# A recurrence whose running minima are spread over the partitions once for all heads, and gates computed as narrow columns

## The chip, the cores and the metric

One core of a Trainium2 chip runs the whole program in one launch. The metric is the device time of that launch in microseconds (us). The engines named below are TensorE (PE, with its weight loads as PEld), VectorE (DVE), ScalarE (ACT), GpSimd (POOL) and SyncE (SP), which issues the weight DMAs.

## The reference, cut to what matters

The model is two layers of one kind (attention, pooling, MLP, on 256 tokens and 256 context tokens) and then two layers of another kind on the 256 tokens, width 1024. The change lies in the second kind alone. Such a layer projects the normalised input to 9232+1024 columns, runs a differential attention with 8 heads (A) and an mLSTM with 8 heads (B), gates both and adds them to the stream. For B the gates are 16 of the projected columns, and the reference is

```
b = cumsum(log_sigmoid(f_pre)); d_log = b[t] - b[s] + ig[s]  (s <= t)
m_t = max(m_prev + b, max_s d_log)
scores = (q @ k.T) * exp(d_log - m_t)
h = (scores @ v + ...) / max(|sum(scores) + ...|, exp(-m_t))
```

It is written by chunks there; the kernel computes the same thing over all 256 tokens at once. With c[s] = ig[s] - b[s], the exponent is c[s] minus the running maximum of c up to t, so that the kernel needs, per head, a column c (by s, on the partitions) and a row of running minima of -c (by t, along the free axis, the same on all partitions), plus a mask that forbids s > t.

## The kernel before, in words

All matrix products of the projections are made in three passes: each float32 matrix is split into a rounded float32r part h and a rest l, and `mm3` (lines 426 to 430) adds l*h, h*h and h*l in PSUM. Weights come as 512 KB pieces in an order that `_order()` writes out (lines 140 to 191); five raw buffers hold them (`RAW`), ScalarE rounds them to `wh` (line 345), VectorE makes the rest `wl` (line 346), and four pieces may stand ready (`RING`). A piece of kind "raw" is taken unsplit and keeps its raw buffer until `W.finish`. The order of the instructions on each engine is made when the program is built, by the framework's scheduler with a simulated timeline and the order of the program text as priority.

The main stream of a layer is `in2(g, ...)`: twenty groups of 512 columns, each with two accumulators of 128 tokens, 8 steps of 2 x 3 matmuls of 512 columns (`group`, lines 479 to 494). After each step `tick()` lets the side generators (class `Sides`) put in a piece of their own work: the attention (lines 1539 to 1602), the gate chain (1477 to 1521), the convolutions (1624 to 1639), the recurrence (1689 to 1741), and `gate_T` (1747 to 1767), which normalises, gates and transposes an attention or recurrence result into the split operand (`oT`, `bT`) of the output products.

Gates (lines 1465 to 1475): the 16 gate columns are one weight piece of 8 steps of 16 columns, split into `wh` and `wl`; per step and token tile there are three matmuls with the activations as the 128x128 stationary operand and 16 columns moving, 48 in all. `chain_gates` turns them into `ccol` (c and exp of the running term, per token) and `nmm` (8 heads x 256 running minima, on 8 partitions).

Recurrence: `stage_s(h)` makes for one head the score products (lines 1698 and 1699, 64 rows of contraction, float32, 256 and 128 columns), and beside them, in a second PSUM bank, the exponent: a product of a one-hot column (`ident[0:8, h]` broadcast to 128) with `nmm` (line 1703, 8 rows, float32), which repeats that head's row on all partitions, and a product of the identity with the mask (line 1704) added to it. Two of each are needed, for the two blocks of s. `stage_e` takes the exponentials from PSUM with `ccol` as the bias (line 1711) and multiplies them with the scores (line 1713). `stage_v(h)`, two steps later, makes three matmuls with `vB` (line 1723), four small VectorE operations for the denominator (1727 to 1730) and two scaled copies into `hb` (1732). The recurrence runs beside `in2(14)`, `in2(12)`, `in2(15)` and `in2(13)`, and so does `gate_T` for the attention's result `oa`.

PSUM: `wk2()` is one buffer of two banks (tag `pr`), `wk_ps()` two buffers of one bank (tag `wk`), the accumulators take the remaining four banks. In SBUF the large tiles (`big`) share ten buffers; `gbuf` is one of them and is needed until the gate chain is done.

Of the kernel before, what the change touches and what calls it, by code (L numbers as in the profile page):

```python
# [26 lines left out]
def _units():  # L27
    u = []
    for i in range(2):
        for s in range(6):  # L30
            for e in range(8):
                u.append((("mod", i, s, e), 1024))
        for g, n in ((0, 416), (1, 448), (2, 448)):
            for h in range(2):
                u.append((("in", i, g, h), 4 * n))
        u.append((("uq", i), 1152))
        u.append((("ukv", i), 768))
        u.append((("pool", i), 128))
        for o in range(2):
            for h in range(2):  # L40
                u.append((("out", i, o, h), 2048))
        for f in range(16):
            u.append((("m1", i, f), 2048))
        for q in range(4):
            for o in range(2):
                for h in range(2):
                    u.append((("m2", i, q, o, h), 2048))
    for i in range(2):
        for g in range(20):
            for h in range(2):  # L50
                u.append((("in2", i, g, h), 2048))
        u.append((("gates", i), 128))
        for nm in ("oa", "ob", "oo"):
            for o in range(2):
                for h in range(2):
                    u.append(((nm, i, o, h), 2048))
    offs, at = {}, 0
    for key, n in u:
        offs[key] = (at, n)
        at += 128 * n  # L60
    return offs, at
# [26 lines left out]
_KC = [("ident", 128), ("mask", 128), ("maskT", 128), ("rope", 192), ("inv", 32), ("sel", 2), ("selg", 2)]  # L88
# [51 lines left out]
def _order():  # L140
# [41 lines left out]
    for i in range(2):  # L182
        def a2(*gs):
            return [("w", ("in2", i, g, h), 4) for g in gs for h in range(2)]
        o += a2(0) + [("w", ("gates", i), 8)] + a2(2, 4, 1, 3, 5)
# [9 lines left out]
def tile_kernel(ctx: ExitStack, tc: tile.TileContext, wp, xall, cols_d, rows_d, brow_d, con_d, band_d, pos_d, out):  # L195
# [91 lines left out]
    def cn(key, n):  # L287
        return con[:, _CON[key]:_CON[key] + n]
# [9 lines left out]
    maskr = const.tile([P, 4, P], F32R, name="maskr")  # L298
# [970 lines left out]
    S.copy(maskr[:, 0:4:2, :], cn("mask", 128).unsqueeze(1).to_broadcast([P, 2, P]))  # L1269
    S.copy(maskr[:, 3, :], cn("maskT", 128))  # L1270
# [104 lines left out]
    def second_layer(i, ent, nxt):  # L1375
# [87 lines left out]
        nmm = smp.tile([8, 256], F32, tag="nmm", name=nm("nmm"), bufs=1)  # L1463
        ccol = smp.tile([P, 2, 2, 8], F32, tag="ccol", name=nm("ccol"), bufs=1)
        pg = wk2()
        pgs = [pg[:, t, :] for t in range(2)]
        for k in range(8):
            w = W.kt(("gates", i))
            h, l = ent.view(k)
            for t in range(2):  # L1470
                mm3(pgs[t][:, 0:16], (h[:, t * P:(t + 1) * P], l[:, t * P:(t + 1) * P]), w, k == 0, k == 7)
            W.used()
        ug = gbuf[:, 0:32].rearrange("p (t g) -> p t g", t=2)
        for t in range(2):
            V.scalar_tensor_tensor(ug[:, t, :], pgs[t][:, 0:16], rs(t), rw("gb", 16), ALU.mult, ALU.add)

        def chain_gates():
# [6 lines left out]

            fT = ug[:, :, 8:16]
# [132 lines left out]


# [69 lines left out]
        def recurrence():  # L1689
            yield from until(h_gates, h_att1, *convs)  # L1690
            d = {}

            def stage_s(h):
                r0 = 64 * (h % 2)
                ft = h // 2
                pr = wk2()
                ps, pm = pr[:, 0, :], pr[:, 1, :]
                T.matmul(ps[:, 0:256], mqk[r0:r0 + 64, 4 + ft, 0:P], mqk[r0:r0 + 64, ft, 0:256], start=True, stop=True)
                T.matmul(ps[:, 256:384], mqk[r0:r0 + 64, 4 + ft, P:256], mqk[r0:r0 + 64, ft, P:256], start=True, stop=True)
                one = ident[0:8, h:h + 1].to_broadcast([8, P])  # L1700
                for s_ in range(2):
                    c0 = 256 * s_
                    T.matmul(pm[:, c0:c0 + 256 - P * s_], one, nmm[:, s_ * P:256], start=True, stop=False)  # L1703
                    T.matmul(pm[:, c0:c0 + P], identr, maskr[:, 3, :], start=False, stop=True)
                stage_e(h, ps, pm)

            def stage_e(h, ps, pm):
                wt = e4("wt")
                for s_ in range(2):
                    c0 = 256 * s_  # L1710
                    S.activation(wt[:, c0:c0 + 256 - P * s_], pm[:, c0:c0 + 256 - P * s_], AF.Exp, bias=ccol[:, s_, 0, h:h + 1])
                aT = wt[:, 512:1024]
                V.scalar_tensor_tensor(aT[:, 0:384], ps[:, 0:384], 0.125 * 0.25, wt[:, 0:384], ALU.mult, ALU.mult)
                d[h] = aT

            def stage_v(h):
                aT = d[h]
# [15 lines left out]
                del d[h]  # L1733

            for step in range(8 + 2):
                if 0 <= step - 2 < 8:
                    stage_v(step - 2)
                yield 1
                if step < 8:
                    stage_s(step)  # L1740
                yield 1
# [105 lines left out]
def _pack(a):  # L1847
# [46 lines left out]
    for i in range(2):  # L1894
# [9 lines left out]
        put(("gates", i), kt(w[:, 6144:6160]))  # L1904
# [50 lines left out]
    for j in range(4):  # L1955
        for s in range(2):
            con[32 * j + s, _CON["sel"] + s] = 1.0
            con[32 * j + s, _CON["selg"] + s] = 1.0
    con[2, _CON["selg"]:_CON["selg"] + 2] = 1.0
# [30 lines left out]
```

## Time and profile before

| | us |
|---|---|
| median of three runs | 1769.97 |
| lowest and highest run | 1767.61, 1774.82 |
| the profiled execution, its own time | 1766.66 |
| its span, first to last instruction | 1764.7 |
| mean granted TensorE clock, share of full | 0.984 |
| PE busy | 1694.5 (96%) |
| DVE busy | 1025.4 (58%) |
| ACT busy | 855.8 (48%) |
| POOL busy | 331.6 (19%) |

Busy time is the share of the span in which an engine had at least one instruction running. A matmul in the list lasts from its start to its modelled end, so neighbours overlap; the pace of a stream is read from the distances of the starts. A float32 matmul appears as two instructions, a float32r one as one.

### The profile page before, as it was taken

To read this page: it belongs to the slowest core of one execution; us is meant where nothing else is said; L and a number is where in the kernel's file an instruction comes from. 1 tells how busy PE (TensorE), PEld (TensorE's weight loads), DVE (VectorE), ACT (ScalarE), POOL (GpSimd) and SP (SyncE) were. 2 spreads that over 40 slices of the span, in tenths; PEclk is the share of its full clock that TensorE was granted. 3 is DMA by queue.
4 is the path that set the end of the run, shared out by engine and by line. 5 is a ranking of instruction groups with operands and counts; after the bars stand their busy time and mean duration, and the time that the engine had idled before them with its cause. 6 is when DMAs were issued, how large, how long until landed. Compare 5 with 4: busy or idle time off the path is not lost.

```text
span 1764.7 us, 26533 instructions
## 1 busy us (share of the span) xinstructions
PE 1694.5 (96%) x10062; PEld 1362.7 (77%) x10062; DVE 1025.4 (58%) x1882; ACT 855.8 (48%) x1658; POOL 331.6 (19%) x414
## 2 busy tenths in 40 slices
PE   6989999999999999889999999999999999999998
PEld 5776578777778888656899978877778788787787
DVE  3476634333333436774566778776575577866755
ACT  4556534413222234564544465665554446655542
POOL 1134110211112121331122224520000034300000
PEclk9999999999999999999999999999999999999999
DMA  7611254555443322602665545444355444343453
GB/s 285 211 61 54 74 190 125 179 163 166 149 151 118 96 78 77 219 30 81 218 189 184 188 146 167 138 132 156 119 170 188 145 155 154 129 160 119 155 183 104
DMA packets 71999, 256.23 MB, mean 145 GB/s; under 512 B 8120, under 2 KB 9272, under 8 KB 71616
## 3 DMA queue, kind: packets, MB, share of 16 engines
q1 hardware_dynamic: 71856, 254.53, 44.2%
q8 instruction: 79, 1.29, 0.3%
q14 instruction: 48, 0.39, 0.1%
q10 hardware_dynamic: 16, 0.02, 0.0%
HBM read 253.47 MB, written 1.05 MB: 144 GB/s over the span
## 4 chain that ended last, share of the span: by engine, by line
PE 86%; DVE 6%; ACT 3%; DMA 2%; POOL 2%; issue 1%; SPq 0%; DVEq 0%; ACTq 0%; POOLq 0%
PE acc L428 24%; PE acc L430 23%; PE acc L429 23%; PE acc L998 2%; DVE wl L346 2%; PE pr L549 2%; PE wk L1037 1%; DMA raw<-in_dram 1%; PE pr L1024 1%; ACT e L1011 1%; PE pr L1703 1%; PE wk L549 1%; ACT wh L345 1%; PE pr L1553 1%; DVE nmx L1008 1%
## 5 line engine op out<-in xcount | busy, mean ns | idle before, releaser
L346 DVE TENSOR_TENSOR wl<-raw,wh 128x1024 fp32r<-128x1024 f32 (+3 forms) x384 | 478.7, 1249 | 415.5 <-ACT wh L345 414.9
L345 ACT CAST wh<-raw 128x1024 fp32r<-128x1024 f32 (+3 forms) x384 | 396.7, 1034 | 505.2 <-PE acc L430 338.6
L428 PE MATMUL acc<-wl,hh 128*128 128x512 f32 x576 | 231.1, 401 | 4.6 <-ACT tga L1683 2.3
L429 PE MATMUL acc<-wh,hh 128*128 128x512 f32 x576 | 230.5, 400 | 0.0
L430 PE MATMUL acc<-wh,hl 128*128 128x512 f32 x576 | 229.6, 399 | 0.0
L428 PE MATMUL acc<-wl,hidh 128*128 128x512 f32 x384 | 152.5, 398 | 0.0
L429 PE MATMUL acc<-wh,hidh 128*128 128x512 f32 x384 | 151.2, 394 | 0.0
L430 PE MATMUL acc<-wh,hidl 128*128 128x512 f32 x384 | 151.0, 395 | 0.0
L1197 POOL TENSOR_TENSOR sqr<-relu 128x512 f32<-128x512 f32 (+1 forms) x64 | 72.6, 1135 | 346.5 <-ACT relu L1195 233.1
L428 PEld LDWEIGHTS acc<-wl,hh 128*128 128x128 f32 x576 | 109.5, 190 | 28.2 <-ACT tga L1683 3.2
L430 PEld LDWEIGHTS acc<-wh,hl 128*128 128x128 f32 x576 | 109.5, 190 | 22.8 <-issue 1.3
L429 PEld LDWEIGHTS acc<-wh,hh 128*128 128x128 f32 x576 | 109.5, 190 | 22.2 <-issue 1.3
L428 PE MATMUL acc<-hl,wh 128*128 128x258 f32 (+1 forms) x384 | 113.1, 295 | 3.5 <-DVE xc L1627 3.5
L429 PE MATMUL acc<-hh,wh 128*128 128x258 f32 (+1 forms) x384 | 111.6, 291 | 0.0
L430 PE MATMUL acc<-hh,wl 128*128 128x258 f32 (+1 forms) x384 | 111.0, 290 | 0.0
L428 PE MATMUL acc<-h2l,wh 128*128 128x512 f32 (+1 forms) x288 | 108.4, 376 | 2.7 <-DVE dx L1128 2.7
L429 PE MATMUL acc<-h2h,wh 128*128 128x512 f32 (+1 forms) x288 | 108.5, 377 | 0.0
L430 PE MATMUL acc<-h2h,wl 128*128 128x512 f32 (+1 forms) x288 | 107.5, 373 | 0.0
L428 PEld LDWEIGHTS acc<-wl,hidh 128*128 128x128 f32 x384 | 72.2, 188 | 17.8 <-issue 1.8
L430 PEld LDWEIGHTS acc<-wh,hidl 128*128 128x128 f32 x384 | 72.1, 188 | 17.1 <-issue 1.0
L429 PEld LDWEIGHTS acc<-wh,hidh 128*128 128x128 f32 x384 | 72.2, 188 | 16.4 <-issue 0.8
L1130 POOL TENSOR_TENSOR x<-x,dx 128x512 f32<-128x512 f32 x30 | 45.8, 1553 | 198.1 <-DVE dx L1128 198.1
(425 smaller groups left out, 3343.1 us busy)
## 6 DMA issues: line engine op xcount, KB each, us to landing
raw<-in_dram SPq DMA_DIRECT2D x448, 512.0 KB, 3.6
raw<-in_dram SPq DMA_DIRECT2D x16, 448.0 KB, 4.2
raw<-in_dram SPq DMA_DIRECT2D x8, 416.0 KB, 6.0
x<-in_dram SPq DMA_DIRECT2D x2, 1024.0 KB
band<-in_dram SPq DMA_DIRECT2D x4, 512.0 KB
raw<-in_dram SPq DMA_DIRECT2D x4, 288.0 KB, 4.2
out_dram<-x SPq DMA_DIRECT2D x4, 256.0 KB, 2.0
rows<-in_dram SPq DMA_DIRECT2D x4, 232.0 KB, 2.5
```

What stands on the lines that cost most here:

```text
L345: S.copy(h, src)
L346: V.tensor_tensor(l, src, h.bitcast(F32), ALU.subtract)
L428: T.matmul(ps, a[0], b[1], start=start, stop=False)
L429: T.matmul(ps, a[0], b[0], start=False, stop=False)
L430: T.matmul(ps, a[1], b[0], start=False, stop=stop)
L549: T.matmul(ps[32 * j:32 * j + 32, 0:P], cpad[:, k, :], raw[:, k * P:(k + 1) * P], start=a == 0, stop=a == 1)
L998: T.matmul(ps[:, a, s_ * w:(s_ + 1) * w], pr["q"][a][s_], pr["k"][a], start=True, stop=True)
L1008: V.tensor_reduce(nmx, ps.rearrange("p a (q w) -> p (a q) w", q=nq), AX.X, ALU.max, negate=True)
L1011: S.activation(e[:, c * w:(c + 1) * w], pf[:, c * w:(c + 1) * w], AF.Exp, bias=nmx[:, c:c + 1], accum_out=ssum[:, c:c + 1])
L1024: T.transpose(pt[:, a, (k * nq + s_) * P:(k * nq + s_ + 1) * P], d["e"][:, a * 512 + (s_ * nk + k) * P:a * 512 + (s_ * nk + k + 1) * P], i ...
L1130: (V if o else G).tensor_tensor(xs, xs, d, ALU.add)
L1197: G.tensor_tensor(s, t, t, ALU.mult)
```

## The change

The gate weights are padded from 16 to 32 columns and taken raw. They become the stationary operand: four steps of four matmuls with 32 columns of weights each, on the four column groups of the array, with 256 tokens moving (once the h part, once the l part of the activations). The four groups' partial sums lie on 4 x 32 partitions; they are copied out and added and transposed by two products with a small constant `self` (four stacked 16x16 identities), from which the old formula goes on.

A new generator `spread()` runs after the gate chain and the second half of the attention: it splits `nmm` into float32r parts and, for four heads at a time, makes the one-hot products (16 matmuls of 256 columns in all); VectorE adds the mask to the first 128 columns and ScalarE copies the others, into `gB`, a view of `gbuf`, which so stays in use until the last exponentials.

The recurrence works on pairs of heads: `stage_s(ft)` makes the score products of both heads, alternating between partitions 0 to 63 and 64 to 127 and between the two banks; VectorE adds the mask for the second block; ScalarE takes the exponentials from SBUF; one VectorE operation multiplies both heads. The products with the identity and the mask are gone, and the loop has five steps instead of ten.

```diff
-        o += a2(0) + [("w", ("gates", i), 8)] + a2(2, 4, 1, 3, 5)
+        o += a2(0) + [("raw", ("gates", i), 1)] + a2(2, 4, 1, 3, 5)

...
+        gB = gbuf.rearrange("p (h c) -> p h c", h=8)
-        pg = wk2()
-        pgs = [pg[:, t, :] for t in range(2)]
-        for k in range(8):
-            w = W.kt(("gates", i))
-            h, l = ent.view(k)
+
+        g_raw = []
+
+        def gate_weights():
+            g_raw.append((yield from W.take(("gates", i), 0)))
+
+        drain(spawn(gate_weights()))
+        g_w = g_raw[0].rearrange("p (k g) -> p k g", k=8)
+        pg = wk_ps()
+        for n in range(4):
+            for j in range(4):
+                k = 4 * (n // 2) + j
+                T.matmul(pg[32 * j:32 * j + 32, 0:256], g_w[:, k, :], ent.view(k)[n % 2][:, 0:256].bitcast(F32), start=n == 0, stop=n == 3)
+        W.finish(("gates", i), 0)
+        ug = gbuf[:, 0:32].rearrange("p (t g) -> p t g", t=2)
+
+        def gate_columns():
+            gs = gbuf[:, 768:1024]
+            S.copy(gs, pg[:, 0:256])
+            yield 1
+            pt = wk_ps()
-                mm3(pgs[t][:, 0:16], (h[:, t * P:(t + 1) * P], l[:, t * P:(t + 1) * P]), w, k == 0, k == 7)
-            W.used()
-        ug = gbuf[:, 0:32].rearrange("p (t g) -> p t g", t=2)
-        for t in range(2):
-            V.scalar_tensor_tensor(ug[:, t, :], pgs[t][:, 0:16], rs(t), rw("gb", 16), ALU.mult, ALU.add)
+                T.matmul(pt[:, 16 * t:16 * t + 16], gs[:, t * P:(t + 1) * P], cn("self", 16), start=True, stop=True)
+                V.scalar_tensor_tensor(ug[:, t, :], pt[:, 16 * t:16 * t + 16], rs(t), rw("gb", 16), ALU.mult, ALU.add)

...
+            yield from gate_columns()

...
+        def spread():
+
+            yield from until(h_gates, h_att1)
+            nmr = tmp(512, F32R, "nmr")[0:8, :].rearrange("p (b c) -> p b c", b=2)
+            split_into(nmr[:, 0, :], nmr[:, 1, :], nmm)
+            yield 1
+            for p4 in range(2):
+                pb = wk2()
+                for a in range(4):
+                    one = identr[0:8, 4 * p4 + a:4 * p4 + a + 1].to_broadcast([8, P])
+                    for b in range(2):
+                        T.matmul(pb[:, a // 2, 256 * (a % 2):256 * (a % 2) + 256], one, nmr[:, b, :], start=b == 0, stop=b == 1)
+                g4 = gB[:, 4 * p4:4 * p4 + 4, :]
+                b4 = pb.rearrange("p b (a c) -> p (b a) c", a=2)
+                V.tensor_tensor(g4[:, :, 0:P], b4[:, :, 0:P], cn("maskT", 128).unsqueeze(1).to_broadcast([P, 4, P]), ALU.add)
+                S.copy(g4[:, :, P:2 * P], b4[:, :, P:2 * P])
+                yield 2
+
+        h_spread = spawn(spread())
+

...
-            yield from until(h_gates, h_att1, *convs)
+            yield from until(h_spread, *convs)
-            def stage_s(h):
-                r0 = 64 * (h % 2)
-                ft = h // 2
-                pr = wk2()
-                ps, pm = pr[:, 0, :], pr[:, 1, :]
-                T.matmul(ps[:, 0:256], mqk[r0:r0 + 64, 4 + ft, 0:P], mqk[r0:r0 + 64, ft, 0:256], start=True, stop=True)
-                T.matmul(ps[:, 256:384], mqk[r0:r0 + 64, 4 + ft, P:256], mqk[r0:r0 + 64, ft, P:256], start=True, stop=True)
-                one = ident[0:8, h:h + 1].to_broadcast([8, P])
+            def stage_s(ft):
+
+                ps = wk2()
-                    c0 = 256 * s_
-                    T.matmul(pm[:, c0:c0 + 256 - P * s_], one, nmm[:, s_ * P:256], start=True, stop=False)
-                    T.matmul(pm[:, c0:c0 + P], identr, maskr[:, 3, :], start=False, stop=True)
-                stage_e(h, ps, pm)
-
-            def stage_e(h, ps, pm):
-                wt = e4("wt")
-                for s_ in range(2):
-                    c0 = 256 * s_
-                    S.activation(wt[:, c0:c0 + 256 - P * s_], pm[:, c0:c0 + 256 - P * s_], AF.Exp, bias=ccol[:, s_, 0, h:h + 1])
-                aT = wt[:, 512:1024]
-                V.scalar_tensor_tensor(aT[:, 0:384], ps[:, 0:384], 0.125 * 0.25, wt[:, 0:384], ALU.mult, ALU.mult)
-                d[h] = aT
+                    for a in range(2):
+                        r0 = 64 * a
+                        T.matmul(ps[:, a, 256 * s_:256 * s_ + 256 - P * s_], mqk[r0:r0 + 64, 4 + ft, P * s_:P * s_ + P],
+                                 mqk[r0:r0 + 64, ft, P * s_:256], start=True, stop=True)
+                wt = e4("wt").rearrange("p (a c) -> p a c", a=2)
+                V.tensor_tensor(wt[:, :, 256:384], gB[:, 2 * ft:2 * ft + 2, P:2 * P],
+                                cn("maskT", 128).unsqueeze(1).to_broadcast([P, 2, P]), ALU.add)
+                for a in range(2):
+                    h = 2 * ft + a
+                    S.activation(wt[:, a, 0:256], gB[:, h, :], AF.Exp, bias=ccol[:, 0, 0, h:h + 1])
+                    S.activation(wt[:, a, 256:384], wt[:, a, 256:384], AF.Exp, bias=ccol[:, 1, 0, h:h + 1])
+                V.scalar_tensor_tensor(wt[:, :, 0:384], ps[:, :, 0:384], 0.125 * 0.25, wt[:, :, 0:384], ALU.mult, ALU.mult)
+                d[ft] = wt
-                aT = d[h]
+                aT = d[h // 2][:, h % 2, :]

...
-                del d[h]
-
-            for step in range(8 + 2):
-                if 0 <= step - 2 < 8:
-                    stage_v(step - 2)
-                yield 1
-                if step < 8:
+
+            for step in range(4 + 1):
+                if step < 4:
-                yield 1
+                yield 2
+                if step > 0:
+                    for a in range(2):
+                        stage_v(2 * (step - 1) + a)
+                        yield 1

```

Left out above: the constant `self`, the padding of the weights from 16 to 32 columns (the piece grows from 64 to 128 KB) and the mask tile, which loses one of its four parts and the copy that filled it.

## Rows read from the trace of the kernel before

**Rows 1.** the page, parts 1, 4 and 6: engine, chain, weight DMA

```profile
PE 1694.5 (96%) x10062; PEld 1362.7 (77%) x10062; DVE 1025.4 (58%) x1882; ACT 855.8 (48%) x1658; POOL 331.6 (19%) x414
...
PE 86%; DVE 6%; ACT 3%; DMA 2%; POOL 2%; issue 1%; SPq 0%; DVEq 0%; ACTq 0%; POOLq 0%
...
raw<-in_dram SPq DMA_DIRECT2D x448, 512.0 KB, 3.6
```

**Rows 2.** timeline, PE, main stream; start us, us, engine, line, op, tiles

```profile
1204.94 0.39 PE L430 MATMUL acc<-wh,hl 128*128 128x512 f32 x1
...
1211.74 0.39 PE L430 MATMUL acc<-wh,hl 128*128 128x512 f32 x1
```

**Rows 3.** timeline, PE: first head of the recurrence

```profile
1213.10 0.39 PE L430 MATMUL acc<-wh,hl 128*128 128x512 f32 x1
1213.42 0.70 PE L1698 MATMUL pr<-mqk 64*128 64x256 f32 x2
...
1214.27 0.69 PE L1703 MATMUL pr<-nmm,con 8*128 8x256 f32 x2
1214.89 0.33 PE L1704 MATMUL pr<-maskr,identr 128*128 128x128 f32 x1
...
1215.72 0.45 PE L428 MATMUL acc<-wl,hh 128*128 128x512 f32 x1
...
1216.01 0.40 PE L429 MATMUL acc<-wh,hh 128*128 128x512 f32 x1
```

**Rows 4.** timeline, PE: gates, first and last of 48, and what follows

```profile
1054.78 0.17 PE L428 MATMUL pr<-wl,hh 128*128 128x16 f32 x1
...
1059.94 0.26 PE L430 MATMUL pr<-wh,hl 128*128 128x16 f32 x1
...
1060.05 0.61 PE L430 MATMUL acc<-wh,hl 128*128 128x512 f32 x1
```

**Rows 5.** behind the gates; us, PE, PEld, DVE, ACT, POOL busy, PEclk, DMA

```profile
1060.00:1064.00 4.00, 4.00 (x12) 3.18 (x12) 3.93 (x10) 3.49 (x4) 4.00 (x4) 0.57 0.51 165
1422.00:1426.00 4.00, 4.00 (x12) 3.22 (x12) 3.93 (x8) 2.22 (x3) 4.00 (x4) 0.57 0.17 46
```

**Rows 6.** timeline, PE: three products with vB amid the stream

```profile
1646.11 0.40 PE L428 MATMUL acc<-wl,hh 128*128 128x512 f32 x1
1646.35 0.83 PE L1723 MATMUL wk<-vB,wt 128*128 128x129 f32 x6
...
1647.25 0.39 PE L430 MATMUL acc<-wh,hl 128*128 128x512 f32 x1
```

**Rows 7.** timeline, PE: attention scores, two row groups amid the stream

```profile
1090.75 0.39 PE L429 MATMUL acc<-wh,hh 128*128 128x512 f32 x1
1091.07 0.70 PE L1553 MATMUL pr<-kT,qT 64*128 64x256 f32 x4
...
1092.03 0.39 PE L428 MATMUL acc<-wl,hh 128*128 128x512 f32 x1
```

**Rows 8.** timeline, PE: modulation products, four column groups amid the stream

```profile
314.02 0.40 PE L428 MATMUL acc<-h2l,wh 128*128 128x512 f32 x1
314.35 0.64 PE L549 MATMUL pr<-raw,cpad 128*32 128x128 f32 x16
...
315.26 0.39 PE L430 MATMUL acc<-h2h,wl 128*128 128x512 f32 x1
```

**Rows 9.** the same view: recurrence of layer 1, and a later stall of PE

```profile
1213.30:1276.10 62.80, 62.80 (x299) 48.43 (x299) 39.41 (x98) 34.28 (x64) 0.00 (x0) 1.00 0.37 123
...
1302.00:1308.00 6.00, 4.83 (x24) 3.68 (x23) 4.29 (x9) 4.26 (x8) 0.00 (x0) 1.00 0.55 174
```

**Rows 10.** groups by form, DVE, 1205 to 1330 us: the recurrence and gate_T

```profile
L1713 DVE SCALAR_TENSOR_TENSOR wt<-pr,wt 128x384 f32<-128x384 f32 x8 | 4.4, 556 | 11.6 <-ACT wt L1711 11.6
L1760 DVE SCALAR_TENSOR_TENSOR oa<-oa,rs,saz 128x128 f32<-128x128 f32 x16 | 4.4, 347 | 0.0
...
L424 DVE SCALAR_TENSOR_TENSOR oTl<-wk,gang,oTh 128x256 fp32r<-128x256 f32 x8 | 3.8, 475 | 0.0
```

More of the change, by code (lines that the diff above doesn't have):

```diff
@@ L51, in _units @@
                 u.append((("in2", i, g, h), 2048))
-        u.append((("gates", i), 128))
+        u.append((("gates", i), 256))
         for nm in ("oa", "ob", "oo"):
@@ L86 @@
     _NROW += _n
-_KC = [("ident", 128), ("mask", 128), ("maskT", 128), ("rope", 192), ("inv", 32), ("sel", 2), ("selg", 2)]
+_KC = [("ident", 128), ("mask", 128), ("maskT", 128), ("rope", 192), ("inv", 32), ("sel", 2), ("selg", 2), ("self", 16)]
 _CON, _NCON = {}, 0
@@ L297, in tile_kernel @@
     identr = const.tile([P, P], F32R, name="identr")
-    maskr = const.tile([P, 4, P], F32R, name="maskr")
+    maskr = const.tile([P, 3, P], F32R, name="maskr")
     ones = const.tile([P, P], F32, name="ones")
@@ L1268, in tile_kernel @@
     S.copy(identr, ident)
-    S.copy(maskr[:, 0:4:2, :], cn("mask", 128).unsqueeze(1).to_broadcast([P, 2, P]))
-    S.copy(maskr[:, 3, :], cn("maskT", 128))
+    S.copy(maskr[:, 0:3:2, :], cn("mask", 128).unsqueeze(1).to_broadcast([P, 2, P]))
     S.activation(maskr[:, 1, :], ident, AF.Copy, scale=0.0)
@@ L1903, in _pack @@
                     put(("in2", i, g, h), wk_[:, 4 * h:4 * h + 4])
-        put(("gates", i), kt(w[:, 6144:6160]))
+        put(("gates", i), kt(np.concatenate([w[:, 6144:6160], np.zeros((1024, 16), f32)], axis=1)))
         for nm_, key in (("oa", "w_out_a_2"), ("ob", "w_out_b_2"), ("oo", "w_o_2")):
@@ L1958, in _pack @@
             con[32 * j + s, _CON["selg"] + s] = 1.0
+        con[32 * j:32 * j + 16, _CON["self"]:_CON["self"] + 16] = np.eye(16, dtype=f32)
     con[2, _CON["selg"]:_CON["selg"] + 2] = 1.0
```

## Prediction, made before the changed kernel was run

> **What bounds the kernel now.** I read the page first: PE is busy 96% of the span and carries 86% of the chain that ended last [rows 1]. So a microsecond taken from PE's stream is worth about a microsecond, wherever PE doesn't wait, and the question is what the touched pieces cost that stream. The timeline answers it: the side work stands between the matmuls of the main stream, and the distance of the neighbours, less their own pace, is its price. The pace: 30 steps from 1204.94 to 1211.74 us, 0.2267 us for 512 columns in one pass, 0.443 ns a column [rows 2]. The second thing to see is the stretch table behind the gates, where the granted clock is 0.57 [rows 5]. The third is DVE in the recurrence, 39.4 of 62.8 us [rows 9], since DVE is what could take PE's place.
>
> **What a head costs now.** From the L430 at 1213.10 to the L429 at 1216.01 are 2.91 us [rows 3]; two steps of the stream lie in that (0.453), so the head's six products cost 2.46. Sixteen heads (8 in each of two layers): 39.3 us.
>
> **What the gates cost now.** 48 matmuls from 1054.78 to the next of the stream at 1060.05 [rows 4]: 5.27 us a layer, 0.110 us each though only 16 columns move. PE had no gap in it, and yet the clock behind is granted at 0.57 over 4 us in both layers [rows 5], that is partly at the 1.2 GHz level instead of 2.4: 4 x 0.43 = 1.72 us lost a layer.
>
> **Prices of the new products.** Float32, same shape of array as the stream: three products of 129 columns cost 1647.25 - 1646.11 - 0.453 = 0.69 us [rows 6], 1.77 ns a column, four times the stream's 0.443, and nothing on top. Row groups: two products of 256 columns on 64 rows each cost 1092.03 - 1090.75 - 0.453 = 0.83 [rows 7]; one alone would stream 256 x 1.77 = 0.45, so the two run together and 0.37 is paid for the visit. Column groups: eight products of 128 columns with 32 weight columns cost 315.26 - 314.02 - 0.453 = 0.79 [rows 8]; two rounds stream 0.45, so four run together, and the visit costs 0.33. That a visit with another shape costs about 0.35 and one with the same shape nothing fits a rule. The Trainium skill, "TensorEngine Tiling (Array Packing)", Tiling Modes, Key Properties, says that a change of the tiling mode drains TensorE; the trace agrees, with the 0.37 and 0.33 above. It speaks against this change, which makes 14 such visits of its own (8 for scores, 4 to spread, 2 for gates); without it the new work would come out some 5 us cheaper.
>
> **The change, part by part.**
> - Scores: eight pair visits instead of sixteen single ones, each (256 + 128) x 1.77 ns = 0.68, plus 0.37: 1.05, in all 8.4 us.
> - Spreading: 32 products of 256 columns in float32r, in four batches of eight: 8 x 256 x 0.443 ns = 0.91, plus 0.37 = 1.28; in all 5.1 us. A float32r product on 8 rows isn't in the trace. Below, it can't stream faster than the pace, and the batch could miss the 0.37 (3.6 in all); above, the float32 rate makes it 8 x 0.45 + 0.37 = 4.0 a batch, 16.0 in all. I take the low rate, since the operands have the type of the stream.
> - Masks by DVE: the sixteen mask visits are gone with the heads' 2.46.
> - So the recurrence gives 39.3 - 8.4 - 5.1 = 25.8 us. Products with vB and the transposes of gate_T stay, and as same-shape work cost nothing extra wherever they fall.
> - Gates: four rounds of 256 columns, 4 x 0.453 + 0.33 = 2.15 us; then two products of 16 columns, four instructions with 128 weight columns, by the narrow ones' 0.110 each 0.44 (if each made a visit of 0.37 of its own, 1.2). Per layer 5.27 - 2.15 - 0.44 = 2.7, and 1.72 for the clock if it doesn't fall: 4.4, two layers 8.8 us. Between nothing and 1.72 for the clock I take 1.72: the new gate products are of the kind of the modulation visits [rows 8], behind which the stream goes on at its pace (314.92 to 315.26 apart), than to the narrow ones.
> - Off the path: the split of the gate weights (ACT and DVE) goes, the piece grows to 128 KB. It now holds its raw buffer until PE has read it, and the loads behind it on SP's queue wait for that. Four split pieces stand ready, each 12 matmuls x 0.227 = 2.7 us of stream, 10.9 us, against 3.6 us to land [rows 1]. Without that cover: 3.6 us a layer.
> - New waits: the gate chain starts one copy later; its results aren't needed before the attention ends. The recurrence waits for the spreading, which has the last projection groups ahead of the recurrence to run beside; the second batch waits until DVE and ACT have emptied the first (under 1 us each by the 0.475 for 256 columns [rows 10]), with PE's stream going on. Both products with vB wait for one multiplication of both heads; four ticks lie between, some 5 us of stream, against about four exponentials and 1.1 us on DVE. If that is late, PE stands, with the whole stream behind it.
> - DVE in the recurrence: eight multiplications of 556 ns become four of at most twice that (no change), and four mask additions of about 475 ns come on top [rows 10]: 41.3 us. PE's stretch shrinks by 8 x 2.46 - 4 x 1.05 = 15.4 to 47.4 us, so DVE goes from 63% to 87%. In that state PE lost 6.0 - 4.83 = 1.17 us later [rows 9]; I book one more such stall a layer, 2.3 us.
>
> Sum: 25.8 + 8.8 - 2.3 = 32.3 us. The profiled execution took 1766.66 us, 3.3 less than the median of the runs shown. 1766.7 - 32.3 = 1734.4; against the median 1738.
>
> **The rivals.**
> - *DVE becomes the bound of the recurrence.* Over 47.4 us a layer, DVE's order fills up and gate_T's share, 16 x 0.347 + 8 x 0.475 = 9.4 us [rows 10], falls to PE as waits: 18.7 us instead of 2.3, 1754. For it: 87%, and splits for the stream in the same queue. Against it: four pieces stand ready, and gate_T isn't needed until the output product, four groups later. Chance 0.13.
> - *The groups don't run together* (the change doesn't do what it says): each pair 0.68 more, each gate stage 12 x 0.453 = 5.4 more: 5.4 + 10.9 = 16.3, 1754. Rows 7 and 8 show both together [rows 7, 8], so 0.04.
> - *The clock falls all the same*, behind the gates and behind the spreading too, in both layers: 4 x 1.72 = 6.9, 1745. Chance 0.08. The Trainium skill, "TensorE: Matmul & The Clock Gate", Part 1, puts a fall of the clock down to idleness; by that the gates, which left no gap, wouldn't be its cause, and 3.4 of these us would stay lost. The rows differ from it, as far as busy time shows.
> - *Slower: the buffers.* `gbuf` lives until the last exponentials. Beside it stand the two halves of the input, oa, mqk, vB, saz, hb and the gate tile: nine of ten; the first half of `oT` takes the tenth, so that the second finds no buffer until `gbuf` or `mqk` is free. If that comes later than `in2(19)`, both gate_T passes run alone in front of the output products: per head 2 x 0.347 + 2 x 0.475 = 1.64 one after the other, 13.2 a pass, 26.3 a layer, 52.6 in all: 34.6 - 52.6 = 18 slower, 1788. It decides only if the last pair slips past `in2(16)` to `in2(19)`, four groups of 48 x 0.227 = 10.9 us; with the recurrence some 47 us long it should be done before these begin. Chance 0.04.
>
> **How the numbers follow.** Forecast 0.71, the rivals 0.13, 0.04, 0.08 and 0.04. The forecast's own range is 1726 (no stall, float32r batches without the 0.37, hidden column products, run to run some us) to 1746 (a second stall, part of the spreading at the float32 rate). To leave out no more than 2 in 10 it reaches to 1753, most of the way to the DVE rival. Half a per cent, 8.8 us, is about what a measurement of this kernel can tell from no change. All cases but the last are over that; with mixtures of the DVE case: faster 0.92, within 0.04, slower 0.04.
>
> **What would show it.** Right: PE's busy time lower by about 30 us; a pair visit of about 1.05 us and a spreading batch of about 1.3 in the timeline; the gate stage near 2.6 us with the clock at 1.00 behind it; DVE above 80% in the recurrence, PE's waits up by a few us. Wrong: waits of PE for `wl` or `wt` of over 10 us; a pair visit near 1.7; or a first `oT` half that comes only after the recurrence, with PE standing at the output product.

## The result, and the profile after

The changed kernel took 1741.28 us in the median of four runs (1738.86 to 1744.13), the kernel before, beside it on the same chip, 1768.79 (1766.45 to 1774.82). The ratio on record is 0.9833, with a 95% interval from 0.9811 to 0.9856: faster by 1.4 to 1.9%, some 25 to 33 us (the two medians by themselves give 0.9844, 27.5 us). The forecast was 1738.0, the range 1726 to 1753.

The page of the profile of the changed kernel, parts 1 and 4, answers to [rows 1]:

```profile
span 1738.9 us, 26348 instructions
...
PE 1666.3 (96%) x9974; PEld 1341.6 (77%) x9974; DVE 1026.5 (59%) x1886; ACT 859.6 (49%) x1663; POOL 331.9 (19%) x414
...
PE 85%; DVE 6%; ACT 3%; DMA 2%; issue 2%; POOL 1%; SPq 0%; DVEq 0%; ACTq 0%; POOLq 0%
```

PE is busy 28.2 us less, and the bound is the same: 96% of the span, 85% of the chain. The timeline of PE in the changed kernel (start, length, engine, line, operation, tiles), first a spreading batch, then a pair of heads, answers to [rows 3]:

```profile
1208.46 0.39 PE L430 MATMUL acc<-wh,hl 128*128 128x512 f32 x1
1208.78 1.22 PE L1644 MATMUL pr<-nmr,identr 8*128 8x256 f32 x8
1209.93 0.50 PE L428 MATMUL acc<-wl,hh 128*128 128x512 f32 x1
1210.27 0.40 PE L429 MATMUL acc<-wh,hh 128*128 128x512 f32 x1
...
1216.87 0.39 PE L428 MATMUL acc<-wl,hh 128*128 128x512 f32 x1
1217.19 0.92 PE L1733 MATMUL pr<-mqk 64*128 64x256 f32 x8
1218.04 0.50 PE L429 MATMUL acc<-wh,hh 128*128 128x512 f32 x1
1218.38 0.40 PE L430 MATMUL acc<-wh,hl 128*128 128x512 f32 x1
```

Two steps of the stream (0.453) lie in each. The batch costs 1210.27 - 1208.46 - 0.453 = 1.36 us (forecast 1.28), the pair 1218.38 - 1216.87 - 0.453 = 1.06 (forecast 1.05); the other pairs and batches that stand by themselves cost the same within 0.01. The gates of layer 1, in the same view, answer to [rows 4]:

```profile
1054.74 0.39 PE L430 MATMUL acc<-wh,hl 128*128 128x512 f32 x1
1055.06 0.38 PE L1395 MATMUL wk<-lp,ones 64*128 64x2 f32 x2
1055.37 0.64 PE L1477 MATMUL wk<-hh,raw 128*32 128x256 f32 x8
...
1056.35 0.50 PE L428 MATMUL acc<-wl,hh 128*128 128x512 f32 x1
...
1057.02 0.42 PE L1477 MATMUL wk<-hl,raw 128*32 128x256 f32 x3
...
1058.71 0.42 PE L1477 MATMUL wk<-hh,raw 128*32 128x256 f32 x3
...
1060.04 0.39 PE L429 MATMUL acc<-wh,hh 128*128 128x512 f32 x1
```

The 16 products don't stand together: the scheduler put steps of the stream between them, so three visits pay the change of array shape. From 1054.74 to 1060.04 are 5.30 us; eight steps of the stream (1.81) and the older L1395 products (0.40, to 1055.37) lie in that. That leaves 3.1 us instead of 2.15; in layer 2 two visits cost 2.7. Behind them the clock is granted in full, where it was 0.57 [rows 5]; the stretch table of the changed kernel (us, busy PE, PEld, DVE, ACT, POOL, PEclk, DMA), the recurrence last, which answers to [rows 9]:

```profile
1060.00:1064.00 4.00, 4.00 (x19) 3.25 (x19) 1.94 (x6) 3.97 (x8) 2.20 (x5) 1.00 0.38 131
...
1408.00:1412.00 4.00, 4.00 (x20) 3.32 (x20) 4.00 (x6) 1.20 (x2) 4.00 (x4) 1.00 0.74 263
...
1213.30:1276.10 62.80, 62.80 (x321) 51.56 (x320) 47.96 (x116) 41.30 (x73) 0.00 (x0) 1.00 0.48 158
```

PE has no gap in the recurrence, though DVE rose from 39.4 to 48.0 us in a stretch of 62.8.

**A ledger without the start.** The medians hide where the difference lies, because the first layers, which the change hardly touches, take from 1035 to 1043 us from profile to profile. So each profile is cut where the third layer begins (the first L428 on `wl,hh`); behind that point, PE's idle time is summed over twenty equal stretches, and the clock loss as PE's busy time times (1 - PEclk). These sums are the measure of the experiments (us but for the ratio):

```
kernel                   median ratio  until cut  behind it  idle  clock loss
before                       -          1035.1     729.6     18.1    10.3
before again (e5)            -          1036.6     729.4     17.8    10.4
gates alone (e1)           0.9969       1039.8     723.4     19.2     6.2
recurrence alone (e2)      0.986        1040.3     702.6     15.8    10.6
after                      0.9833       1038.5     700.4     21.9     6.0
after again (e11)          0.9831       1037.5     700.7     19.2    10.3
softmax by ACT (e3)        0.9817       1038.4     700.0     18.1     8.1
head by head (e4)          0.9827       1040.3     702.8     21.0    10.4
mask by GpSimd (e6)        0.9823       1036.8     700.2     21.4     4.8
mask twice by DVE (e7)     0.982        1038.7     700.6     19.2    10.2
gates behind group 2 (e8)  0.9802       1041.6     697.8     18.9     9.3
e3 and e8 together (e9)    0.9763       1040.8     690.1     14.3     3.9
gates before group 5 (e10) 0.9765       1042.9     690.2     15.6     3.9
e3 and e10 together (e12)  0.9799       1041.8     693.6     18.3     2.5
```

The change is worth 29.2 us behind the cut, the forecast 32.3. Two profiles of the same program agree there within 0.3 us; idle time and clock loss trade against each other between them (21.9 and 6.0, 19.2 and 10.3), so only their sum is compared below. e4, whose products cost PE the same, stands 2.1 to 2.4 us above them, so a difference of that size between one profile each of two kernels shows nothing. What is called PE's waits in the attention and the convolutions below is its idle time from a layer's beginning to its first scores of the recurrence, without the waits for `hh` and `hl` at the beginning.

### The profile page after: what moved, and what is told of

It reads as the page before. It is cut to its first block, busy times and chain, and to the rows that moved or that the text cites. A ratio compares the mean times of both kernels' runs of the same rounds, so it can differ in the third digit from the quotient of the medians.

```text
span 1738.9 us, 26348 instructions
## 1 busy us (share of the span) xinstructions
PE 1666.3 (96%) x9974; PEld 1341.6 (77%) x9974; DVE 1026.5 (59%) x1886; ACT 859.6 (49%) x1663; POOL 331.9 (19%) x414
## 3 DMA queue, kind: packets, MB, share of 16 engines
HBM read 253.61 MB, written 1.05 MB: 146 GB/s over the span
## 4 chain that ended last, share of the span: by engine, by line
PE 85%; DVE 6%; ACT 3%; DMA 2%; issue 2%; POOL 1%; SPq 0%; DVEq 0%; ACTq 0%; POOLq 0%
PE acc L428 24%; PE acc L429 24%; PE acc L430 23%; PE acc L998 2%; PE pr L549 2%; DVE wl L346 1%; DMA raw<-in_dram 1%; PE wk L1037 1%; PE pr L1024 1%; ACT e L1011 1%; PE wk L549 1%; PE pr L1567 1%; ACT wh L345 1%; DVE nmx L1008 1%; PE wk L1752 1%
## 5 line engine op out<-in xcount | busy, mean ns | idle before, releaser
L346 DVE TENSOR_TENSOR wl<-raw,wh 128x1024 fp32r<-128x1024 f32 (+2 forms) x382 | 475.0, 1246 | 411.3 <-ACT wh L345 410.8
L345 ACT CAST wh<-raw 128x1024 fp32r<-128x1024 f32 (+2 forms) x382 | 395.8, 1037 | 491.4 <-PE acc L430 327.3
L428 PE MATMUL acc<-wl,hh 128*128 128x512 f32 x576 | 229.2, 398 | 3.6 <-ACT tga L1717 2.6
L428 PE MATMUL acc<-wl,hidh 128*128 128x512 f32 x384 | 152.7, 398 | 0.0
L428 PEld LDWEIGHTS acc<-wl,hh 128*128 128x128 f32 x576 | 108.3, 188 | 27.7 <-ACT tga L1717 3.1
L428 PE MATMUL acc<-hl,wh 128*128 128x258 f32 (+1 forms) x384 | 113.0, 294 | 1.2 <-DVE xc L1661 1.2
L428 PE MATMUL acc<-h2l,wh 128*128 128x512 f32 (+1 forms) x288 | 108.7, 377 | 2.7 <-DVE dx L1128 2.7
L428 PEld LDWEIGHTS acc<-wl,hidh 128*128 128x128 f32 x384 | 72.1, 188 | 17.7 <-issue 1.8
```

The source lines that it names most:

```text
L345: S.copy(h, src)
L346: V.tensor_tensor(l, src, h.bitcast(F32), ALU.subtract)
L428: T.matmul(ps, a[0], b[1], start=start, stop=False)
```

## The experiments

**e1, gates alone.** The kernel before with the gate part of the change.

```diff
-                mm3(pgs[t][:, 0:16], (h[:, t * P:(t + 1) * P], l[:, t * P:(t + 1) * P]), w, k == 0, k == 7)
...
+                T.matmul(pg[32 * j:32 * j + 32, 0:256], g_w[:, k, :], ent.view(k)[n % 2][:, 0:256].bitcast(F32), start=n == 0, stop=n == 3)
```

> The kernel before with the new gates alone (narrow columns, raw weights), the old recurrence. Theory A (the gates' gain is partly swallowed: PE reaches the convolutions earlier and waits there for a chain of GpSimd work that is as long as before): the clock is 1.00 behind the gates, but the time is only 2 to 5 us under the kernel before, PE standing 5 us or more a layer around the convolutions. Rival B (the gates earn all that was forecast, and the recurrence falls short because of VectorE): 8 to 9 us under the kernel before.

Measured: 1766.74 us against 1773.15, ratio 0.9969 (0.9952 to 0.9986), so 2 to 9 us; in the ledger 6.2. The interval spans both theories' numbers; the profile is clearer: clock loss 4.1 us lower, idle time 1.1 higher. PE's waits in the attention and the convolutions are 4.7 and 5.2 us in the two layers, 4.0 and 3.4 in the kernel before: theory A's picture, at about its size.

**e2, recurrence alone.** The kernel before with the spreading and the pairs.

```diff
-            yield from until(h_gates, h_att1, *convs)
+            yield from until(h_spread, *convs)
...
-                one = ident[0:8, h:h + 1].to_broadcast([8, P])
...
+                wt = e4("wt").rearrange("p (a c) -> p a c", a=2)
```

> The kernel before with the new recurrence and spreading alone, the old gates. Theory A: 24 to 26 us under the kernel before (ratio about 0.986), the clock behind the gates still near 0.57 for 4 us. Rival B: the recurrence is worth only some 19 us (0.989), with PE's waits in it up by 5 us or more.

Measured: 1747.71 us, ratio 0.986 (0.9832 to 0.9888), so 20 to 30 us; in the ledger 27.0. That is near theory A, and PE's idle time fell from 18.1 to 15.8 us, where the rival had it rise by 5. With the gates of 16 columns kept, the clock loss stays at 10.6. The stretches behind the gates in e2 show why:

```profile
1064.00:1068.00 4.00, 4.00 (x20) 3.47 (x20) 3.90 (x12) 2.52 (x3) 3.39 (x2) 0.69 0.36 135
1412.00:1416.00 4.00, 4.00 (x23) 3.61 (x24) 3.67 (x11) 1.84 (x3) 3.84 (x4) 0.71 0.40 131
```

and the same in e1:

```profile
1064.00:1068.00 4.00, 4.00 (x20) 3.34 (x20) 3.96 (x6) 3.42 (x6) 3.89 (x3) 1.00 0.38 120
1420.00:1424.00 4.00, 4.00 (x19) 3.33 (x18) 3.46 (x6) 2.77 (x4) 3.59 (x4) 1.00 0.81 251
```

The windows cut the lower stretch differently, so that the mean of 4 us is 0.57 in one kernel and 0.69 in the other. The level is the same: 0.50, that is 1.2 GHz, in e2 as between 1060.40 and 1063.60 us in the kernel before. Here is e2 up to the end of its gates and behind them:

```profile
1055.00:1065.60 10.60, 10.60 (x72) 9.46 (x71) 7.16 (x21) 7.23 (x11) 6.22 (x15) 1.00 0.38 129
1065.70:1068.90 3.20, 3.20 (x9) 2.55 (x8) 3.13 (x10) 3.17 (x4) 3.20 (x3) 0.50 0.31 95
```

So the lower clock goes with the old gate products of 16 columns, and goes away with them. A wait of 1.2 us for `hh` at the beginning of layer 1 went away with them too, but it isn't the cause: in layer 2 such waits (0.9 us for `hh`, 1.5 for `hl`) stand ahead of the gates in e1 as in e2. The Trainium skill, "TensorE: Matmul & The Clock Gate", Part 1, ties the clock to how busy TensorE has been recently. PE's busy time is 10.60 of the 10.60 us ahead of the lower stretch, so the rows differ from the rule as far as busy time shows.

**e4, another order of the score products.**

```diff
-                for s_ in range(2):
-                    for a in range(2):
+                for a in range(2):
+                    for s_ in range(2):
```

> The changed kernel with the score products of a pair issued head by head instead of alternating between the two row groups. If the row groups run together only when neighbours in the order lie on different groups: a pair visit grows from 1.06 to about 1.5 us (256 columns more of float32 stream), some 3.6 us in all over the changed kernel. Rival D (the groups run together whatever the order, or not at all): the visit stays at 1.06 and the time within 1.5 us.

Measured: 1743.79 us, ratio 0.9827 (0.9792 to 0.9861). The pair in e4's timeline:

```profile
1218.56 0.39 PE L428 MATMUL acc<-wl,hh 128*128 128x512 f32 x1
1218.88 0.93 PE L1733 MATMUL pr<-mqk 64*128 64x256 f32 x8
1219.74 0.50 PE L429 MATMUL acc<-wh,hh 128*128 128x512 f32 x1
1220.08 0.40 PE L430 MATMUL acc<-wh,hl 128*128 128x512 f32 x1
```

1220.08 - 1218.56 - 0.453 = 1.07 us, the same. The edit did reach PE: in the program as built the four products stand head by head. Yet between 1218.88 and 1219.41 us the view by form shows only products of 256 columns, which are the first ones of both heads (two instructions each):

```profile
L1733 PE MATMUL pr<-mqk 64*128 64x256 f32 x4 | 0.7, 428 | 0.0
```

So the second head's first product, third in order, runs beside the first head's, ahead of the first head's second one. The order of issue doesn't decide whether the two row groups run together, and they do: all eight instructions take 0.93 us, where 2 x (256 + 128) columns one after the other would stream 1.36. The ledger has e4 2.1 to 2.4 us above the changed kernel, all of it in idle time and clock loss (31.4 against 27.9 and 29.5); the medians show no difference.

**e5, the kernel before once more.**

> The kernel before, unchanged, profiled once more. Its first profile reached the second layers 3.4 to 5.2 us earlier than the profiles of the changed kernel and of its two halves, with a granted clock of 1.00 between 15 and 45 us where the others show 0.87 to 0.97. If that is scatter of the first stage from one execution to the next (theory A), this profile starts its first recurrent layer between 1036 and 1041 us, with a clock below 1.00 somewhere between 15 and 45 us. If the change itself disturbs the start (theory B), it is again at 1035 us with 1.00.

Measured: 1767.96 us; the third layer begins at 1036.6. The stretches of e5 at the start:

```profile
15.00:30.00 15.00, 12.48 (x94) 8.34 (x95) 11.25 (x38) 9.85 (x30) 5.26 (x16) 0.91 0.96 346
30.00:45.00 15.00, 14.33 (x181) 12.33 (x179) 3.50 (x11) 5.16 (x16) 0.00 (x0) 0.98 0.42 147
```

The clock is below 1.00 in the unchanged kernel too, so the later start is at least in part scatter. Whether all of it is stays open: the unchanged kernel's two profiles give 1035.1 and 1036.6, all others 1036.8 and more.

**e6 and e7, VectorE in the recurrence.** e6 moves the second mask addition of a pair to GpSimd, e7 does it twice.

```diff
-                V.tensor_tensor(wt[:, :, 256:384], gB[:, 2 * ft:2 * ft + 2, P:2 * P],
+                G.tensor_tensor(wt[:, :, 256:384], gB[:, 2 * ft:2 * ft + 2, P:2 * P],
```

> The changed kernel with the second mask addition of each pair visit moved from VectorE to GpSimd. Theory A: TensorE's stream is the bound of the recurrence and VectorE, though nearly full there, isn't; taking about 0.5 us of VectorE work per pair away gives nothing (ratio 0.982 to 0.985, as for the changed kernel). Rival: VectorE is the bound; then 4 x 0.5 us per layer come back, 4 us in all, ratio 0.981 or less, and VectorE falls below 90% in the middle of the recurrence.

> The changed kernel with that mask addition done twice on VectorE, once into columns that nobody reads. Theory A: VectorE has some 6 us to spare over a recurrence of 47 us and the extra 2 us a layer are taken up, at most one more short wait of TensorE: ratio 0.983 to 0.986. Rival: VectorE is at its limit, all 4 us show, and the waits for split weights grow by as much as the additions: ratio 0.986 or more, waits of TensorE beside the recurrence and gate_T up by 4 us.

Measured: e6 1743.86 us, ratio 0.9823 (0.9797 to 0.9849), 700.2 behind the cut; e7 1742.29, ratio 0.982 (0.9796 to 0.9845), 700.6. Taking the work away gives nothing, doubling it costs nothing. e6's interval by itself would leave room for its rival's 4 us; the ledger and e7's interval don't. The stretches of e7 show how near the edge that is:

```profile
1218.00:1224.00 6.00, 6.00 (x33) 4.72 (x33) 5.91 (x10) 4.34 (x7) 0.00 (x0) 1.00 0.49 176
1224.00:1230.00 6.00, 6.00 (x37) 4.84 (x36) 5.67 (x29) 3.57 (x9) 0.00 (x0) 1.00 0.31 95
1230.00:1236.00 6.00, 6.00 (x30) 4.89 (x29) 6.00 (x19) 4.67 (x7) 0.00 (x0) 1.00 0.25 84
1236.00:1242.00 6.00, 6.00 (x34) 4.81 (x33) 5.66 (x8) 2.80 (x3) 0.00 (x0) 1.00 0.74 238
```

VectorE is full for some 24 us, PE without a gap beside it: nothing that PE needs in them comes late.

**e3 and e8, the chains behind the attention.** After the gates had become shorter, PE waited more where the attention passes into the convolutions. The stretches of the changed kernel:

```profile
1134.00:1140.00 6.00, 2.27 (x15) 1.48 (x13) 5.29 (x9) 3.04 (x7) 6.00 (x5) 1.00 0.52 162
1140.00:1146.00 6.00, 4.99 (x26) 4.75 (x27) 4.90 (x11) 1.90 (x4) 5.95 (x7) 0.72 0.04 16
1146.00:1152.00 6.00, 4.46 (x38) 4.04 (x36) 6.00 (x11) 2.88 (x4) 2.15 (x7) 1.00 0.00 0
1152.00:1158.00 6.00, 5.89 (x36) 5.89 (x37) 4.69 (x13) 2.26 (x4) 4.78 (x12) 0.72 0.53 175
```

In the first of them PE works 2.27 of 6 us while GpSimd is full, and the clock falls behind it. The chain of waits there runs through GpSimd:

```profile
1132.75 2.91 POOL e L1588 x2
1135.66 1.95 POOL rq L1426
1137.61 1.88 POOL rp L524 x2
1139.49 1.49 POOL rq L1426
1140.98 0.07 issue
1141.05 1.63 POOL rs L1426
```

L1588 scales half of the softmax, L1426 takes the roots for q and k, L524 is part of their rotation. From 1142.72 us on the chain runs mostly through VectorE (convolutions and rotation), to 1152. e3 moves L1588 to ScalarE; e8 moves the gates one group later (of its edit the order of the weights is shown, the block of the gates moves likewise), so that the first q and k chains start earlier beside the stream.

```diff
-                    G.tensor_scalar(e[:, 384 + a:384 + b], e[:, 384 + a:384 + b], r2[:, 2 * qt + 1:2 * qt + 2], None, ALU.mult)
+                    S.activation(e[:, 384 + a:384 + b], e[:, 384 + a:384 + b], AF.Copy, scale=r2[:, 2 * qt + 1:2 * qt + 2])
```

> The changed kernel with one edit: the scaling of the second map's exponentials in the attention goes from GpSimd to ScalarE (two operations a head). Theory A (a row of GpSimd operations is what PE waits for around the convolutions): 3 to 6 us under the changed kernel, and PE's idle time there, 7.0 us in layer 1 and 5.2 in layer 2, falls by at least 2 us each. Rival C (VectorE, which is full there, is the bound): no change within 1.5 us, and the idle time stays.

```diff
-        o += a2(0) + [("raw", ("gates", i), 1)] + a2(2, 4, 1, 3, 5)
+        o += a2(0, 2) + [("raw", ("gates", i), 1)] + a2(4, 1, 3, 5)
```

> The changed kernel with the gates behind group 2 instead of group 0 (and their weight piece moved likewise). Nothing is added or removed. If the shorter gate stage lost part of its gain because the chains of q and k on ACT, DVE and GpSimd did not get shorter with TensorE's stream (theory A), the place of the gates only shifts which wait takes it: TensorE's waits in the attention and the convolutions stay at 5 to 7 us a layer, ratio 0.982 to 0.985. If the loss comes from the gate chain standing in front of the first q chain (theory B), the waits fall to the 3 to 4 us of before and the ratio to about 0.980.

Measured: e3 1740.28 us, ratio 0.9817 (0.9791 to 0.9842), e8 1740.57, ratio 0.9802 (0.9777 to 0.9827). Against the changed kernel that is nothing certain: the ledger gives 0.4 and 2.6 us. In e3 the time is what rival C said. The waits in the attention and the convolutions, 3.7 and 4.6 us in e3, 4.9 and 3.7 in e8, decide nothing: the changed kernel's own two profiles have 7.0 and 5.2, and 5.1 and 4.6. So e8 stays undecided between its two theories.

**e11, e9, e10: the same, together and further.** e11 is the changed kernel again, e9 has both edits of e3 and e8, e10 has the gates ahead of group 5 (`a2(0, 2, 4, 1, 3) + [("raw", ("gates", i), 1)] + a2(5)`, with the block of the gates moved likewise).

> The changed kernel, unchanged, as the measure for the two others of this call on the same chip: a ratio to the kernel before of 0.981 to 0.986, waits of TensorE in the attention and the convolutions of 5 to 7 us a layer.

> Gates behind group 2, and the scaling of the second softmax half by ScalarE instead of GpSimd. Theory (the chains of q, k and softmax are the last wait in the attention, and TensorE's stream is too short beside them): the two reliefs add up, waits of 3 to 4 us a layer, 3 to 5 us less than the changed kernel beside it. Rival: ScalarE, which takes on 16 x 2 scalings, becomes late itself in the attention; then no gain over the changed kernel (within 1.5 us).

> The gates moved to stand ahead of the last group of the attention's projections (group 5), where TensorE afterwards waits most. Theory: the 2.6 us of gate products then fill waiting time; waits of 2 to 4 us a layer in the attention and the convolutions, 4 to 6 us less than the changed kernel beside it. Rival: the gate chain, some thirty small operations on VectorE and ScalarE, then stands amid the convolutions and delays them and the softmax: waits of 6 us a layer or more and no gain.

Measured beside each other: e11 1742.64 us, ratio 0.9831 (0.9811 to 0.985); e9 1730.92, 0.9763 (0.9743 to 0.9782); e10 1730.59, 0.9765 (0.9743 to 0.9786). e11 is as expected. The two others are 12 us under it, two to four times what was expected. In the ledger e9 is 10.6 us under e11, and its idle time and clock loss are 18.2 against 29.5, 11.3 less: that is all of the gain. In e10 they are 19.5; its waits in the attention and the convolutions are 1.4 us in layer 2, but 6.5 in layer 1, as its rival had it, and the gain came all the same. The stretches of e9 at the place shown above:

```profile
1134.00:1140.00 6.00, 3.52 (x26) 2.66 (x25) 6.00 (x12) 4.32 (x8) 3.11 (x5) 1.00 0.50 169
1140.00:1146.00 6.00, 5.32 (x43) 5.09 (x43) 5.96 (x13) 1.19 (x2) 6.00 (x7) 1.00 0.02 8
1146.00:1152.00 6.00, 5.37 (x43) 4.70 (x42) 6.00 (x13) 3.72 (x7) 5.19 (x12) 1.00 0.00 1
1152.00:1158.00 6.00, 6.00 (x43) 5.28 (x43) 6.00 (x13) 3.20 (x6) 2.92 (x9) 1.00 0.56 185
```

PE still waits, but less (3.8 of 24 us, 6.4 before it), and the clock stays at 1.00 in all four. The expected size counted waits alone, not the clock behind them. How much each gave stays open: against e11 the idle time is 4.9 us lower and the clock loss 6.4, against the changed kernel's first profile 7.6 and 2.1. Where the two edits, each alone, come to 0.4 and 2.6 us under the changed kernel in the ledger, they come to 10.3 in one kernel; that the clock loss goes only when the waits are short enough fits the rows, but was not tried by itself.

**e12, e10 with the softmax by ScalarE.**

> Both reliefs that worked in one kernel: the gates ahead of group 5, and the scaling by ScalarE. Theory (each takes waits of its own out of the attention's end): idle time and clock loss behind the first stage, 18 to 19 us in each of the two kernels before it, fall by 3 to 6 us more, ratio about 0.974. Rival (both take away the same wait, TensorE standing before the convolutions, which can go only once): ratio 0.976 to 0.978 as for either alone.

Measured: 1737.83 us, ratio 0.9799 (0.9781 to 0.9817): 7 us over e10's median, the two intervals just overlapping, which neither theory named. The ledger shows 3.4 of them behind the cut, 1.3 in idle time and clock loss (20.8 against 19.5). By the shapes in its timeline, PE leaves the stream's 128*128 44 times behind 1035 us, in e10 39 times; 5 x 0.35 = 1.75 us of the rest may be visits that the scheduler split. The other 3.8 us of the medians are not in these profiles: e10's was taken of its slowest execution, with the latest start of all (1042.9).

## Why the prediction held

- **What bounds the kernel**: right. PE carries the chain as before, 85% of it against 86%.
- **Prices of the products**: right for the recurrence. With 1.06 a pair and 1.36 a batch, 16 x 2.46 - 8 x 1.06 - 4 x 1.36 = 25.4 us come out, against 25.8. The float32r rate nearly holds with 8 rows (the products of a batch start 0.12 us apart, the pace gives 0.113 for 256 columns), and the visit is paid; the 4.0 a batch of the upper bound is far off.
- **The visits**: mis-counted. The Trainium skill, "TensorEngine Tiling (Array Packing)", Tiling Modes, Key Properties, says that a change of the tiling mode drains TensorE; the trace agrees, a pair paying 1.06 - 0.68 = 0.38 us above its streaming. But that visits speak against this change didn't come out: by the shapes in the timeline, PE leaves the stream's 128*128 58 times behind 1035 us in the kernel before and 40 times in the changed one. The old one-hot products were visits as well, and more of them, which the 2.46 a head contained. The new work makes 18 of its own, not 14: five of gates (two of them joined to an older L1395 product) and five to spread, since products of the attention split a batch of layer 2.
- **The gates**: mis-sized. "four rounds of 256 columns, 4 x 0.453 + 0.33" supposed one visit; there were three and two, 3.1 and 2.7 us instead of 2.15. The two products of 16 columns cost 0.23 each, 0.46 a layer (forecast 0.44). A stage costs 3.6 and 3.2 us, not near 2.6, and the gates' products give 10.5 - 5.8 - 0.9 = 3.8 us instead of 5.4. Where the scheduler kept the sixteen together the term holds: in e9 they cost 2.07.
- **The clock behind the gates**: right as a mechanism. e1 and e2 divide it cleanly, and behind the gates the 3.44 us forecast came back; e1's 4.1 in all are those and 0.7 elsewhere. The reason given for it was misread: behind the modulation visits the stream doesn't go on at its pace, 314.92 to 315.26 are 0.34 us and not 0.227. But the gain wasn't kept: in the changed kernel idle time and clock loss together are 27.9 and 29.5, and 28.4 before. Its second profile has the lower level for ten microseconds where the attention passes into the convolutions:

```profile
1136.00:1146.00 10.00, 8.80 (x37) 8.00 (x38) 8.28 (x16) 3.56 (x7) 8.97 (x11) 0.50 0.23 81
```

  PE's waits in the attention and the convolutions, 4.0 and 3.4 us before and 4.1 and 3.4 in e2, are 4.7 and 5.2 in e1 and 7.0 and 5.2 in the changed kernel (5.1 and 4.6 in its second profile), so they came with the gates. That they came because a shorter stream met q, k and softmax chains of the same length is argued, not shown: e8 did not tell it from a gate chain that stands ahead of the first q chain. "its results aren't needed before the attention ends" was true of the gate chain; the prediction didn't ask what had been covered by the 5.3 us of gates that it took out. The halves show it too: 6.2 us in e1 and 27.0 in e2 make 33.2, both together 29.2 and 28.9.
- **DVE in the recurrence**: mis-sized. 87% was forecast, and above 80% named as a sign; from the first scores to the last product with vB DVE is busy 41.6 of 53.1 us in layer 1, 78%, and 77% in layer 2. It is full in the first half alone, which the mean hid (the kernel before, then the changed one in two parts):

```profile
1213.40:1284.00 70.60, 70.60 (x337) 55.02 (x337) 44.46 (x110) 39.69 (x73) 0.00 (x0) 1.00 0.36 121
...
1217.20:1241.20 24.00, 24.00 (x128) 19.12 (x128) 23.55 (x62) 16.05 (x29) 0.00 (x0) 1.00 0.43 140
1241.20:1270.30 29.10, 29.10 (x151) 24.69 (x150) 18.03 (x41) 16.47 (x27) 0.00 (x0) 1.00 0.49 164
```

- **The booked stalls**: wrong in place and cause. "I book one more such stall a layer, 2.3 us" took the 1.17 us of the kernel before for DVE's doing; the row says that PE waited for ScalarE's `tga`:

```profile
1304.78 0.51 PE L428 MATMUL acc<-wl,hh 128*128 128x512 f32 x1 [1.17 <-ACT tga L1683]
```

  The two waits of this kind went away in e2, and the changed kernel has one of 2.6 us in layer 2 and none in layer 1. No stall came from DVE in the recurrence. That the amount was nearly right by the waits in the attention, which had not been named, is luck.

The sum by its measured terms: 25.4 + 3.8 = 29.2 from products, and 28.4 - 27.9 = 0.5 from waits and clock, 29.7 against the 29.2 of the ledger (with the second profile 28.1 against 28.9); the forecast had 31.2 from products, 3.4 from the clock and -2.3 from stalls. So the mechanism of the products carried the forecast, and the clock's gain and the stalls, both not as forecast, nearly cancelled. The start of the program, later by 3.4 us in this profile, makes the span's own difference only 25.8.

Of the rivals, DVE as the bound fell by e6 and e7, the groups apart by the pair's 1.06, the clock behind the gates by e1. The buffers did not decide: the last pair of layer 1 stands at 1239.57 and the first transposes for `oT` at 1234.00, both in the recurrence's first half; both parts of `oT` are written from 1237.3 us on, and its product begins at 1316.4.

```profile
1234.00 0.27 PE L1793 MATMUL wk<-con,oa 128*128 128x128 f32 x1
...
1239.57 0.92 PE L1733 MATMUL pr<-mqk 64*128 64x256 f32 x8
```

## What to carry to other kernels

Price work on the bounding engine by the distance of its neighbours less their pace, and count the visits in the order that the scheduler makes, not in the program's. When a piece of the bounding stream is taken out, ask which chains on the other engines ran under its cover: here the gates' saving was 6 us alone and 2 us beside the new recurrence, of 8.8 forecast, until the gates were moved one group later together with a relief of the softmax chain, or ahead of the last group, and then 12 us came at once. Cut profiles at a landmark behind which they can be compared; the start alone scattered by more than the size of an edit.

## What the runs showed of the hardware that was not expected

- A clock below full came behind products that left PE no gap: 0.57 over 4 us behind 48 products of 16 columns [rows 5], 0.69 and 0.71 in e2, in each case 0.50 in the middle of the stretch; 1.00 behind 16 products of 256 columns in e1.
- Two row groups overlap whatever the order of issue: 1.06 us a pair alternating, 1.07 one head after the other.
- A float32r product on 8 rows moves 256 columns at nearly the stream's rate: eight in 1.36 us with the change of shape, their starts 0.12 us apart.
